# A hybrid decoder step: GpSimd's two-operand work in the recurrence on VectorE

## The chip, the cores and the metric

The kernel runs on one core of one Trainium2 chip. The metric is the device time of one execution in microseconds (us), the median of several runs. The core's engines are TensorE (PE; its weight loads are listed apart as PEld), VectorE (DVE), ScalarE (ACT), GpSimd (POOL) and SyncE (SP), which issues the DMAs. Each engine takes its own instructions in a fixed order and waits on semaphores for the others.

## The reference

One inference step of a one-layer decoder over a prompt of 1024 tokens and 8 sample tokens, width 1024. All weights and activations are float32. Cut to what matters here:

```python
zall = xn @ w_in                      # 45 column blocks of 128
# time-mix branch, 8 heads x 64, a recurrence over the tokens with a 64x64 state S per head
def _wkv_step(S, inp):
    r, w, k, v, aa, bb = inp
    sa = einsum('bhij,bhj->bhi', S, aa)
    S = S * w[:, :, None, :] + sa[..., :, None] * bb[..., None, :] + v[..., :, None] * k[..., None, :]
    y = einsum('bhij,bhj->bhi', S, r)
    return S, y
y_b = gelu(u) * chunk_spatial(layer_norm(gelu(vb)))       # gMLP branch
merged = sigmoid(m_a) * ((y_a * silu(g_a)) @ w_br_a) + sigmoid(m_b) * ((y_b * silu(g_b)) @ w_br_b)
h = h + merged @ w_out
h = h + sigmoid(h @ w_ple_gate + b) * (p @ w_ple)
y = rms_norm(h) * final_g
```

The prompt's state starts at zero. Each sample token has a stored state of its own and makes one step of the recurrence ("decode").

## The kernel before

**Low parts.** Every large product is made of three matmuls. A float32 operand is split into a rounded high part, which ScalarE copies out, and a low part, which is the operand less the high part: a subtraction with two operands in SBUF. `split` (L111 to L114) does both and takes the engine of the subtraction as an argument. `load_w` (L116 to L127) fetches a weight block in pieces of 128x512, splits each and gives the subtraction to GpSimd. The tags `whi` and `wlo` have three buffers each, and so has `wraw`, the piece as it was fetched. A piece of the next weights can therefore be split only when TensorE has used the last of a buffer.

**Stages.** First the norms, the per-layer projection and the v columns (0 to about 100 us). Then the recurrence (about 100 to 830 us): the prompt is cut into 8 units (4 pairs of heads x 2 halves of the tokens), and each unit into 8 chunks of 64 tokens. Last the merge, the output projection, the gate and the final norm (830 us to the end).

**The recurrence.** For unit `un`, `stage_e` makes the factors: decays, normed keys `e_kn`, key products `m1b` (L663 for the r rows, L665 for the keys), `e_bk`, and splits `e_kp` into `e_rkh` and `e_rkl`. `stage_s` solves a triangular system in 31 steps, each a product into `xtmp` (L737) and an addition into `xg` (L739) on VectorE. `stage_c` is the chain from chunk to chunk: TensorE `pt` (L827), ScalarE `e`, TensorE `pt` (L833), ScalarE `vsb`, TensorE `p3b` (L838), VectorE `vsb` (a SCALAR_TENSOR_TENSOR, recorded at the helper's line L791), and again. `stage_t` finishes a unit.

**Fill.** Between the chain's steps TensorE is given other matmuls: 41 blocks of `w_in` (`zblock`, `ga`, `ugb`, `mgate`) and 8 blocks of `w_br_b` (`br_b`), three matmuls for each 128 rows, all at L138. `Stream.pick` loads the weights of the next block while the present one runs. `ugb` multiplies its result into `mx` (L904). `load_ya` and `load_yb` fetch the branches' inputs back and split them (`xlo`). `lora_w` splits a small weight (`llo`), the branch L530 splits `la`. `sample` is the decode: its four state tiles go in two rounds, in each one on GpSimd and one on VectorE (`E_`, L1015 to L1029).

**Order.** The order on each engine is fixed when the program is built, by a planner that gives an engine the ready instruction of the best priority, by reckoned durations. Instructions of `stage_c` and `stage_t` go through `Boost` and come ahead of all others. The rest goes by the order in which it was written (priority 100000 and up), so a low part has no rank of its own. On the chip an engine keeps that order whatever the durations are.

Of the kernel before, what the change touches and what calls it, by code (L numbers as in the profile page):

```python
# [27 lines left out]
CH = 64  # L28
# [26 lines left out]
def body(tc, A):  # L55
# [7 lines left out]
    with ExitStack() as top:  # L63
# [47 lines left out]
        def split(hi, lo, eng, raw=None):  # L111
            raw = f32(lo) if raw is None else raw
            S.copy(hi, raw)  # L113
            eng.tensor_tensor(lo, raw, f32(hi), ALU.subtract)  # L114

        def load_w(src, nk, pool=None):  # L116
            out = []
            for k0 in range(0, nk, 4):
                n = min(4, nk - k0)
                x = k0 if pool else ""  # L120
                hi = (pool or wp).tile([P, 4, P], F32R, tag=f"whi{x}", name="whi")[:, :n]
                lo = (pool or wp).tile([P, 4, P], F32R, tag=f"wlo{x}", name="wlo")[:, :n]
                raw = (pool or wp).tile([P, 4, P], F32, tag="wraw", name="wraw", bufs=WRAW)[:, :n]
                SY.dma_start(raw, src[:, k0:k0 + n, :])
                split(hi, lo, G, raw)
                out += [(hi[:, k], lo[:, k]) for k in range(n)]
            return out  # L127

# [370 lines left out]
        def zblock(b, mk):  # L499
            def gen(w):  # L500
                z = mk()
                G.memset(z[:, 0:1], 0.0)

                def ev(n, ns, ps):
                    S.copy(z[:, 1 + n * W3:1 + (n + 1) * W3], ps)
                yield from mm_block(w, xhi, xlo, ev)

                def mix():
                    G.tensor_copy(zsh[:, b], z[:, TP:TP + NB + 1])
                    if b < 12:  # L510
                        zt.setdefault(b % 4, {})[b // 4] = z
                    mu = col("mu", b)
                    for n in (2, 1, 0):
                        c0 = 1 + n * W3
                        c1 = c0 + W3
                        d = r2.tile([P, W3], F32, tag="zd", name="zd")
                        e1 = min(c1, TP + 1)
                        V.tensor_tensor(d[:, :e1 - c0], z[:, c0 - 1:e1 - 1], z[:, c0:e1], ALU.subtract)
                        if n == 2:
                            V.tensor_tensor(d[:, e1 - c0:], shs[:, b], z[:, TP + 1:], ALU.subtract)  # L520
                        V.scalar_tensor_tensor(z[:, c0:c1], d, mu, z[:, c0:c1], ALU.mult, ALU.add)
                    if b < 12:
                        G.tensor_copy(zsm[:, (1, 0, 2)[b // 4], b % 4], z[:, TP + 1:])
                    else:
                        S.activation(z[0:64, 1:], z[0:64, 1:], AF.Tanh)
                        G.tensor_copy(wdas, z[:, TP + 1:])
                        for q, x, E_ in ((Q[0], lw, V), (Q[1], la, G)):
                            oq = Q[1 - q.start // 64]
                            S.copy(x[q], z[q, 1:])
                            E_.tensor_tensor(x[oq], z[q, 1:], f32(x[q]), ALU.subtract)  # L530
                if b // 4 != 1:
                    return mix
                mix()
            j, x = b % 4, b // 4
            go = {0: lambda: st.r_seen >= 2 * j, 1: lambda: st.k_seen >= 2 * j, 2: lambda: st.c_seen >= 2 * j - 4,
                  3: lambda: True}[x]
            st.add(("z", b), b, gen, ready=go if x != 1 else lambda: st.it >= 2 * j - 3, go=go)
# [38 lines left out]
        def lora_w(j):  # L576
# [4 lines left out]
                    SY.dma_start(raw[Q[h], x], A["wup"][x * 64:x * 64 + 64, js])  # L581
            S.copy(lhi, raw)
            for x in range(2):
                G.tensor_tensor(llo[Q[x], x], raw[Q[x], x], f32(lhi[Q[x], x]), ALU.subtract)

        sgat, zt, ut, fin_s, tl = {}, {}, {}, {}, {}
        ybh, ybl = xhi[:, 0:4], xlo[:, 0:4]
# [2 lines left out]
        def stage_e(un):  # L590
# [54 lines left out]
            V.scalar_tensor_tensor(kp, zr[:, hs], col("r_k", j), kp, ALU.mult, ALU.mult)  # L645
            rkh = re_.tile([P, HT], F32R, tag="e_i", name="e_rkh")
            rkl = re_.tile([P, HT], F32R, tag="e_a", name="e_rkl")
            split(rkh, rkl, G, kp)
            yield YE[2]
            st.until(("z", 8 + j))  # L650
            if un == 0:
# [5 lines left out]
            for b0 in (0, 4):  # L657
# [2 lines left out]
                    yield 1  # L660
                for h in range(2):
                    q = Q[h]
                    G.tensor_tensor(m1[q, cs, h, RC[h]], c64(zr[q, hs])[:, cs], p65[q, cs, 1:], ALU.mult)  # L663
                    for b in range(2):
                        (G, V)[h].tensor_tensor(kord(m1[q, cs, h, AC[h]], b), perm(c64(kn[q])[:, cs], b),  # L665
                                                perm(p65[q, cs, 0:CH], b), ALU.mult)
                if b0:
                    st.r_seen += 1
                ps = aps().rearrange("p (c h x) -> p c h x", h=2, x=CH)
# [222 lines left out]
        def ugb(j, part):  # L892
            def gen(w):
# [3 lines left out]
                def ev(n, ns, ps):  # L897
# [3 lines left out]
                    else:  # L901
                        S.activation(ue, ps, AF.Tanh, scale=0.5)
                        V.scalar_tensor_tensor(ue, ue, 1.0, ps, ALU.add, ALU.mult)
                    G.tensor_tensor(mx[:, ns], mx[:, ns], ue, ALU.mult)  # L904
                yield from mm_block(w, xhi, xlo, ev)
                SY.dma_start(d_yb[j], mx)
            st.add(("u", j, part), (17 if part == 0 else 25) + j, gen)
# [20 lines left out]
        def sample():  # L928
# [83 lines left out]
            yl = sa_(P, 32, tag="s_yl")  # L1012
            for r in range(2):
                it = []
                for x, E_ in enumerate((G, V)):  # L1015
                    isl, s_ = sst[2 * r + x]
                    t_ = re_.tile([P, 8, HD], F32, tag=("e_a", "e_p")[x], name="s_t")
                    sa8 = r2.tile([P, 8], F32, tag="s_sa", name="s_sa")
                    E_.tensor_tensor(t_, s_, bi(lv[:, NKK]), ALU.mult)
                    it.append((E_, isl, s_, t_, sa8))  # L1020
                yield YS[0]
                for E_, isl, s_, t_, sa8 in it:
                    V.tensor_reduce(sa8, t_, AX.X, ALU.add)
                    E_.tensor_tensor(s_, s_, bi(lv[:, WV]), ALU.mult)
                    E_.tensor_tensor(t_, bj(sa8), bi(lv[:, BV]), ALU.mult)
                    E_.tensor_tensor(s_, s_, t_, ALU.add)
                    E_.tensor_tensor(t_, bj(lvv[:, isl]), bi(lv[:, KP]), ALU.mult)
                    E_.tensor_tensor(s_, s_, t_, ALU.add)
                    E_.tensor_tensor(t_, s_, bi(lv[:, RV]), ALU.mult)  # L1029
                yield YS[1]  # L1030
                for E_, isl, s_, t_, sa8 in it:
                    V.tensor_reduce(yl[:, isl], t_, AX.X, ALU.add)
                yield 1
                while r == 0 and st.cdone < 7 * HCH + 3:
                    yield 1
# [36 lines left out]
        def load_ya(n):  # L1072
            ns = slice(n * W3, min((n + 1) * W3, TP))
            st.load = SY.dma_start(f32(yal[:, :3, ns]), d_ya[:3, :, ns].rearrange("k p t -> p k t")).ins
            for k in range(3):
                st.later.append(lambda k=k, ns=ns: split(yah[:, k, ns], yal[:, k, ns], G))

        def load_yb(n):
            V, S, G_ = (Boost(e) for e in (nc.vector, nc.scalar, nc.gpsimd))
            ns = slice(n * W3, (n + 1) * W3)  # L1080
            SY.dma_start(f32(ybl[:, :, ns]), d_yb[:, :, ns].rearrange("k p t -> p k t"))
            for k in range(4):
                S.copy(ybh[:, k, ns], f32(ybl[:, k, ns]))
                (G_ if k == 1 else V).tensor_tensor(ybl[:, k, ns], f32(ybl[:, k, ns]), f32(ybh[:, k, ns]), ALU.subtract)

        def br_b(j):
            def gen(w):
# [11 lines left out]
        fill += [lambda j=j: mgate(37 + j, d_mb[j]) for j in range(KD)]  # L1099
        fill += [lambda j=j: mgate(29 + j, d_ma[j]) for j in range(KD)]  # L1100

        tc.cur_priority = 100000
        boost[0] = 50000
        zblock(12, lambda: re_.tile([P, T + 1], F32, tag="zr", name="wda"))
# [61 lines left out]
            pass  # L1166
        repool.__exit__(None, None, None)
        rw.close()
        use_pmm(4)

        tr2 = top.enter_context(tc.tile_pool(name="tr2", bufs=2))
# [219 lines left out]
```

## Time and profile before

| what | value |
|---|---|
| median of 3 runs | 1077.36 us (1076.85 to 1077.84) |
| the profiled execution | 1079.88 us, of which the profiled span is 1078.0 us |
| TensorE busy | 1016.7 us (94%) |
| VectorE busy | 655.1 us (61%) |
| GpSimd busy | 471.6 us (44%) |
| ScalarE busy | 449.3 us (42%) |
| granted TensorE clock, mean | 0.978 of full |

A busy figure sums the instructions' own durations; an instruction that is held by something inside it counts as busy. Idle time of an engine is put down to what released the instruction behind it. A group of instructions is written as line, engine, operation, output<-inputs, shapes, count, then busy time and mean duration, then the idle time before them.

### The profile page before, as it was taken

Reading aid. Unit: us, or ns where it says so; the run is one execution under the profiler, and the core shown is the slowest. Engines: PE = TensorE matmul, PEld = TensorE weight load, DVE = VectorE, ACT = ScalarE, POOL = GpSimd, SP = SyncE. Lnnn points to the kernel's source line nnn. Section 1 sums busy time; section 2 is a strip of 40 time slices with the busy share of each in tenths; the row PEclk is TensorE's granted clock in tenths of the full one; section 3 lists DMA queues with packets and bytes.
Section 4 is the critical chain, followed back from the end, with each engine's and each line's share of the span. In section 5 each row is a group of like instructions: output and inputs, shape, how many; then the busy total and the mean of one; then the engine's idle time right before and its main releaser. Section 6 shows DMA issues by size and latency. Waiting matters only on the chain. (4 is left out here: it accounts for less than half of the span.)

```text
span 1078.0 us, 17989 instructions
## 1 busy us (share of the span) xinstructions
PE 1016.7 (94%) x6590; PEld 978.4 (91%) x6590; DVE 655.1 (61%) x1487; ACT 449.3 (42%) x1087; POOL 471.6 (44%) x484
## 2 busy tenths in 40 slices
PE   8889999899798999989998999999899999999996
PEld 8768898899798899989998999989799999999995
DVE  6898565847648768577476583563876551114544
ACT  4531334245364453555444545434532232225431
POOL 2462665444364343343414333334943674453213
PEclk9999999999899999999998999999899999999997
DMA  9811412152224231132232332422765763224204
GB/s 277 243 51 48 145 40 58 40 131 83 79 78 151 79 86 61 47 103 56 79 110 49 105 101 70 134 86 41 266 206 179 240 231 118 79 83 133 80 1 157
DMA packets 95224, 118.72 MB, mean 110 GB/s; under 512 B 40672, under 2 KB 61024, under 8 KB 95136
## 3 DMA queue, kind: packets, MB, share of 16 engines
q1 hardware_dynamic: 95136, 117.57, 35.5%
q8 instruction: 52, 0.85, 0.3%
q14 instruction: 36, 0.29, 0.1%
HBM read 84.75 MB, written 32.25 MB: 109 GB/s over the span
## 5 line engine op out<-in xcount | busy, mean ns | idle before, releaser
L138 PE MATMUL mm<-xhi,wlo 128*128 128x344 f32 x1176 | 388.2, 330 | 8.0 <-POOL wlo L114 6.2
L138 PE MATMUL mm<-xlo,whi 128*128 128x344 f32 x1176 | 389.3, 331 | 0.9 <-DVE xlo L791 0.8
L138 PE MATMUL mm<-xhi,whi 128*128 128x344 f32 x1176 | 388.7, 331 | 0.4 <-DVE mb L1092 0.3
L114 POOL TENSOR_TENSOR wlo<-wraw,whi 128x512 fp32r<-128x512 f32 x130 | 171.2, 1319 | 217.6 <-ACT whi L113 215.6
L138 PEld LDWEIGHTS mm<-xhi,wlo 128*128 128x128 f32 x1176 | 225.1, 191 | 10.5 <-POOL wlo L114 7.3
L138 PEld LDWEIGHTS mm<-xlo,whi 128*128 128x128 f32 x1176 | 224.9, 191 | 3.0 <-DVE xlo L791 1.7
L138 PEld LDWEIGHTS mm<-xhi,whi 128*128 128x128 f32 x1176 | 224.9, 191 | 2.6 <-DVE mb L1092 0.6
L113 ACT CAST whi<-wraw 128x512 fp32r<-128x512 f32 x130 | 80.2, 619 | 61.8 <-PE mm L138 44.4
L737 DVE TENSOR_TENSOR xtmp<-nb,xg 128x48 f32<-128x48 f32 (+23 forms) x248 | 70.6, 285 | 20.4 <-DMA nb<-d_n 13.6
L739 DVE TENSOR_TENSOR xg<-xg,xtmp 128x48 f32<-128x48 f32 (+23 forms) x248 | 78.0, 315 | 7.6 <-DVE xtmp L737 0.2
L791 ACT ACTIVATE sp<-vsb,pc 64x64 f32<-64x64 f32 x128 | 44.2, 345 | 69.6 <-DVE vsb L791 67.7
L791 DVE SCALAR_TENSOR_TENSOR vsb<-p3b,pc,sp 64x64 f32<-64x64 f32 x112 | 31.6, 282 | 57.5 <-PE p3b L838 55.3
L827 PEld LDWEIGHTS pt<-vsb,m1b 128*128 128x128 f32 x256 | 37.9, 194 | 28.0 <-DVE vsb L791 27.5
L138 PE MATMUL mm<-hlo,whi 128*128 128x388 f32 (+1 forms) x192 | 62.0, 323 | 0.0
L138 PE MATMUL mm<-hhi,whi 128*128 128x388 f32 (+1 forms) x192 | 61.7, 321 | 0.0
L138 PE MATMUL mm<-hhi,wlo 128*128 128x388 f32 (+1 forms) x192 | 61.7, 321 | 0.0
L138 PE MATMUL mm<-mgl,whi 128*128 128x344 f32 x192 | 61.4, 320 | 0.2 <-POOL mgl L1188 0.2
L827 PE MATMUL pt<-vsb,m1b 128*128 128x64 f32 x256 | 40.4, 275 | 22.4 <-DVE vsb L791 22.4
L138 PE MATMUL mm<-mgh,whi 128*128 128x344 f32 x192 | 61.3, 319 | 0.0
L138 PE MATMUL mm<-mgh,wlo 128*128 128x344 f32 x192 | 61.3, 319 | 0.0
L1202 DVE SCALAR_TENSOR_TENSOR h<-mm,xres 128x344 f32<-128x344 f32 x24 | 12.4, 517 | 75.0 <-PE mm L138 72.6
L791 ACT COPY vsb<-pt 64x64 f32<-64x64 f32 x128 | 26.5, 207 | 43.7 <-PE pt L833 41.7
(297 smaller groups left out, 1881.5 us busy)
## 6 DMA issues: line engine op xcount, KB each, us to landing
wraw<-w_in SPq DMA_DIRECT2D x82, 256.0 KB, 2.8
d_ple<-st_ple SPq DMA_DIRECT2D x8, 516.0 KB, 3.4
d_yb<-mx SPq DMA_DIRECT2D x8, 516.0 KB, 2.8
d_mb<-st_m SPq DMA_DIRECT2D x8, 516.0 KB, 3.4
d_ma<-st_m SPq DMA_DIRECT2D x8, 516.0 KB, 4.1
mb<-d_mb SPq DMA_DIRECT2D x8, 516.0 KB, 4.3
d_tb<-mb SPq DMA_DIRECT2D x8, 516.0 KB, 4.9
ma<-d_ma SPq DMA_DIRECT2D x8, 516.0 KB, 5.3
```

The lines of the kernel that those rows point to most:

```text
L113: S.copy(hi, raw)
L114: eng.tensor_tensor(lo, raw, f32(hi), ALU.subtract)
L138: PE.matmul(ps, l, r, start=(k == 0 and i == 0), stop=(k == nk - 1 and i == 2))
L737: V.tensor_tensor(tv, row.unsqueeze(2).broadcast_to([P, 2, na, w]), xg[:, :, :na, s:s + 1].broadcast_to([P, 2, na, w]), ALU.mult)
L739: V.tensor_tensor(xg[:, :, :na, s + 1:], xg[:, :, :na, s + 1:], tv, ALU.add)
L791: r = f(*a, **k)
L827: PE.matmul(pt[:, 0, h], m1[:, c, h], vs[:, c, h], start=True, stop=True)
L1202: V.scalar_tensor_tensor(h[:, j, ns], ps, 0.25, xr[:, ns], ALU.mult, ALU.add)
```

## The change

All low parts, branch products, key products and the decode's second state that GpSimd made between the start of the recurrence and its end are given to VectorE. `load_w` takes its engine from a list that is set to VectorE ahead of the recurrence and back to GpSimd behind it, so the weight blocks of the last stage stay as they were. What stays on GpSimd in the recurrence: the powers (`rpow`, L101), the scaling of `e_s` (L605), memsets, and copies.

```diff
+        sub = [G]
...
-                split(hi, lo, G, raw)
+                split(hi, lo, sub[0], raw)
...
-                        for q, x, E_ in ((Q[0], lw, V), (Q[1], la, G)):
+                        for q, x in ((Q[0], lw), (Q[1], la)):
...
-                            E_.tensor_tensor(x[oq], z[q, 1:], f32(x[q]), ALU.subtract)
+                            V.tensor_tensor(x[oq], z[q, 1:], f32(x[q]), ALU.subtract)
...
-                G.tensor_tensor(llo[Q[x], x], raw[Q[x], x], f32(lhi[Q[x], x]), ALU.subtract)
+                V.tensor_tensor(llo[Q[x], x], raw[Q[x], x], f32(lhi[Q[x], x]), ALU.subtract)
...
-            split(rkh, rkl, G, kp)
+            split(rkh, rkl, V, kp)
...
-                    G.tensor_tensor(m1[q, cs, h, RC[h]], c64(zr[q, hs])[:, cs], p65[q, cs, 1:], ALU.mult)
+                    V.tensor_tensor(m1[q, cs, h, RC[h]], c64(zr[q, hs])[:, cs], p65[q, cs, 1:], ALU.mult)
                     for b in range(2):
-                        (G, V)[h].tensor_tensor(kord(m1[q, cs, h, AC[h]], b), perm(c64(kn[q])[:, cs], b),
-                                                perm(p65[q, cs, 0:CH], b), ALU.mult)
+                        V.tensor_tensor(kord(m1[q, cs, h, AC[h]], b), perm(c64(kn[q])[:, cs], b),
+                                        perm(p65[q, cs, 0:CH], b), ALU.mult)
...
-                    G.tensor_tensor(mx[:, ns], mx[:, ns], ue, ALU.mult)
+                    V.tensor_tensor(mx[:, ns], mx[:, ns], ue, ALU.mult)
...
-                for x, E_ in enumerate((G, V)):
+                for x in range(2):
...
-                    E_.tensor_tensor(t_, s_, bi(lv[:, NKK]), ALU.mult)
+                    V.tensor_tensor(t_, s_, bi(lv[:, NKK]), ALU.mult)
...
-                st.later.append(lambda k=k, ns=ns: split(yah[:, k, ns], yal[:, k, ns], G))
+                st.later.append(lambda k=k, ns=ns: split(yah[:, k, ns], yal[:, k, ns], V))
...
-                (G_ if k == 1 else V).tensor_tensor(ybl[:, k, ns], f32(ybl[:, k, ns]), f32(ybh[:, k, ns]), ALU.subtract)
+                V.tensor_tensor(ybl[:, k, ns], f32(ybl[:, k, ns]), f32(ybh[:, k, ns]), ALU.subtract)
...
+        sub[0] = V
         tc.cur_priority = 100000
         boost[0] = 50000
...
         rw.close()
+        sub[0] = G
         use_pmm(4)
```

## Rows read from the trace of the kernel before

**Rows 1.** Busy by stretch: PE, PEld, DVE, ACT, POOL, granted clock, DMA.

```profile
100.00:215.00 115.00, 106.14 (x696) 101.58 (x695) 75.66 (x152) 42.06 (x91) 60.47 (x77) 0.99 0.25 77
215.00:745.00 530.00, 505.66 (x3467) 491.35 (x3467) 337.56 (x893) 256.99 (x699) 209.29 (x231) 0.98 0.31 88
745.00:830.00 85.00, 76.72 (x477) 72.97 (x476) 63.90 (x107) 33.93 (x93) 49.17 (x36) 0.96 0.57 189
...
880.00:1078.00 198.00, 187.73 (x1197) 186.72 (x1195) 64.89 (x113) 62.78 (x119) 75.42 (x69) 0.97 0.30 101
```

**Rows 2.** Waits of TensorE over the span: us in total, times, longest us.

```profile
PE pt L827 <- DVE vsb L791: 22.4, 19, 5.5
PE mm L138 <- POOL wlo L114: 6.2, 4, 2.4
...
PE aa L671 <- DVE e_bk L641: 3.7, 1, 3.7
...
PE mm L138 <- POOL zr L502: 1.8, 1, 1.8
```

**Rows 3.** Timeline of TensorE, its longest wait: start, us, what, idle before.

```profile
283.50 0.90 PE L827 MATMUL pt<-vsb,m1b 128*128 128x64 f32 x3 [5.51 <-DVE vsb L791]
```

**Rows 4.** Timeline of VectorE in the 11.5 us ahead of that wait's end.

```profile
273.51 2.17 DVE L739 TENSOR_TENSOR xg<-xg,xtmp 128x48 f32<-128x48 f32 x1
275.61 1.77 DVE L641 SCALAR_TENSOR_TENSOR e_bk<-e_a,e_i 128x512 f32<-128x512 f32 x1
...
278.86 1.41 DVE L665 TENSOR_TENSOR m1b<-e_kn,e_p 64x128 f32<-64x128 f32 x1
280.30 1.16 DVE L737 TENSOR_TENSOR xtmp<-nb,xg 128x48 f32<-128x48 f32 x1
281.50 0.83 DVE L739 TENSOR_TENSOR xg<-xg,xtmp 128x48 f32<-128x48 f32 x1
...
283.17 0.59 DVE L791 SCALAR_TENSOR_TENSOR vsb<-p3b,pc,sp 64x64 f32<-64x64 f32 x2
```

**Rows 5.** Timeline of GpSimd in the same stretch.

```profile
271.60 1.44 POOL L663 TENSOR_TENSOR m1b<-zr,e_p 64x256 f32<-64x256 f32 x2 [2.20 <-DVE xg L739]
273.11 1.58 POOL L665 TENSOR_TENSOR m1b<-e_kn,e_p 64x128 f32<-64x128 f32 x2
...
275.54 1.28 POOL L114 TENSOR_TENSOR wlo<-wraw,whi 128x512 fp32r<-128x512 f32 x1
...
281.36 0.90 POOL L904 TENSOR_TENSOR mx<-mx,ue 128x344 f32<-128x344 f32 x1
```

**Rows 6.** TensorE by stretch, behind and ahead of that wait: busy (matmuls), clock, DMA.

```profile
283.50:289.50 6.00, 6.00 (x23) 0.50 0.61 191
269.50:275.50 6.00, 6.00 (x44) 1.00 0.00 0
```

**Rows 7.** Groups of GpSimd by shape, 100 to 815 us.

```profile
L114 POOL TENSOR_TENSOR wlo<-wraw,whi 128x512 fp32r<-128x512 f32 x87 | 115.1, 1326 | 152.4 <-ACT whi L113 150.8 <-PE mm L138 0.9
...
L101 POOL TENSOR_TENSOR s_pool<-s_pool,mhalf 128x16 f32<-128x16 f32 x2 | 5.9, 2952 | 11.7 <-DVE s_pool L925 11.7
```

**Rows 8.** Groups of the page, the two operations of the triangular solve.

```profile
L737 DVE TENSOR_TENSOR xtmp<-nb,xg 128x48 f32<-128x48 f32 (+23 forms) x248 | 70.6, 285 | 20.4 <-DMA nb<-d_n 13.6
L739 DVE TENSOR_TENSOR xg<-xg,xtmp 128x48 f32<-128x48 f32 (+23 forms) x248 | 78.0, 315 | 7.6 <-DVE xtmp L737 0.2
```

**Rows 9.** Single lines of VectorE: duration ns min/median/max, starts, forms.

```profile
L739 DVE TENSOR_TENSOR xg<-xg,xtmp x248: 166/224/2174, 190.3 to 725.9; 128x48 f32<-128x48 f32 x12, 128x54 f32<-128x54 f32 x8, 128x84 f32<-128x84 f32 x8, 128x56 f32<-128x56 f32 x8
...
L665 DVE TENSOR_TENSOR m1b<-e_kn,e_p x32: 384/788/1976, 150.6 to 670.8; 64x128 f32<-64x128 f32 x32
...
L641 DVE SCALAR_TENSOR_TENSOR e_bk<-e_a,e_i x8: 682/1116/1774, 151.4 to 644.3; 128x512 f32<-128x512 f32 x8
...
L700 DVE TENSOR_TENSOR w3b<-aa,mka x32: 405/417/419, 165.5 to 683.2; 64x256 f32<-64x256 f32 x32
...
L518 DVE TENSOR_TENSOR zd<-zr x12: 498/508/1412, 143.3 to 573.8; 128x344 f32<-128x344 f32 x8, 128x336 f32<-128x336 f32 x4
```

More of the change, by code (lines that the diff above doesn't have):

```diff
@@ L1018, in sample @@
                     sa8 = r2.tile([P, 8], F32, tag="s_sa", name="s_sa")
-                    E_.tensor_tensor(t_, s_, bi(lv[:, NKK]), ALU.mult)
-                    it.append((E_, isl, s_, t_, sa8))
+                    V.tensor_tensor(t_, s_, bi(lv[:, NKK]), ALU.mult)
+                    it.append((isl, s_, t_, sa8))
                 yield YS[0]
-                for E_, isl, s_, t_, sa8 in it:
+                for isl, s_, t_, sa8 in it:
                     V.tensor_reduce(sa8, t_, AX.X, ALU.add)
[L1024 to L1029, printed above, removed]
+                    V.tensor_tensor(s_, s_, bi(lv[:, WV]), ALU.mult)
+                    V.tensor_tensor(t_, bj(sa8), bi(lv[:, BV]), ALU.mult)
+                    V.tensor_tensor(s_, s_, t_, ALU.add)
+                    V.tensor_tensor(t_, bj(lvv[:, isl]), bi(lv[:, KP]), ALU.mult)
+                    V.tensor_tensor(s_, s_, t_, ALU.add)
+                    V.tensor_tensor(t_, s_, bi(lv[:, RV]), ALU.mult)
                 yield YS[1]
-                for E_, isl, s_, t_, sa8 in it:
+                for isl, s_, t_, sa8 in it:
                     V.tensor_reduce(yl[:, isl], t_, AX.X, ALU.add)
@@ L1075, in load_ya @@
             for k in range(3):
-                st.later.append(lambda k=k, ns=ns: split(yah[:, k, ns], yal[:, k, ns], G))
+                st.later.append(lambda k=k, ns=ns: split(yah[:, k, ns], yal[:, k, ns], V))
         def load_yb(n):
-            V, S, G_ = (Boost(e) for e in (nc.vector, nc.scalar, nc.gpsimd))
+            V, S = (Boost(e) for e in (nc.vector, nc.scalar))
             ns = slice(n * W3, (n + 1) * W3)
```

## The prediction, made before the changed kernel was run

> **What bounds the kernel now.** I read the busy times by stretch first. TensorE is busy for 505.66 of 530 us in the heart of the recurrence, 76.72 of 85 in its last unit and 187.73 of 198 in the last stage [rows 1]. VectorE stands at 64% of the recurrence (337.56 of 530) and GpSimd at 39%, so neither is the bound by its mean. The change can act only through what TensorE loses between 100 and 830 us: its waits, and the low clock that follows long waits.
>
> The waits come second. 22.4 us in 19 waits go to the chain's VectorE step `vsb`, 6.2 us to low parts of weights from GpSimd, 3.7 us to `e_bk`, 1.8 us to a memset on GpSimd [rows 2]. The granted clock is the second loss: 0.99 of 115 us, 0.98 of 530 and 0.96 of 85 [rows 1] make 1.2 + 10.6 + 3.4 = 15 us. Behind the longest wait the clock reads 0.50 (1.2 GHz), and TensorE makes 23 matmuls in 6 us where it had made 44 at the full 2.4 GHz [rows 6].
>
> Third, the timeline ahead of that longest wait. TensorE stood from 277.99 to 283.50 [rows 3], for a `vsb` that started on VectorE at 283.17 [rows 4]. The timeline shows no idle time of VectorE before it, but its instructions were swollen: an addition of 48 elements took 2.17 us, and the same line takes 0.22 us at the median; `e_bk` took 1.77 against a shortest of 0.68, a key product 1.41 against 0.38, two more of the solve 1.16 and 0.83 [rows 4, 9]. In each of these GpSimd was at a two-operand instruction of its own [rows 5]; one `mx` and two splits like those shown are left out there. The excess of these five is 1.95 + 1.09 + 1.03 + 0.94 + 0.61 = 5.6 us. So VectorE and GpSimd hold one another when both read two operands from SBUF, and the planner's order, in which `vsb` stands behind four steps of the solve that rank below it, fits durations that didn't come about.
>
> **What the change takes away.** The same excess over the whole recurrence: the solve's 496 instructions are busy for 70.6 + 78.0 = 148.6 us [rows 8]; at the median of 0.224 they would take 111 [rows 9], so 38 us are holding. Of the 32 key products on VectorE half take 0.79 or more against 0.38, at least 6 us more; of the eight `e_bk` half take 1.12 or more against 0.68, at least 2 us [rows 9]. That makes 46 us. My estimate for all two-operand lines of VectorE, mean less shortest form by form in the same way, is about 90 us. What stays on GpSimd reads little (powers of 8 or 16 elements, copies), so I take nearly all of it as gone.
>
> **What it adds.** By uncontended VectorE durations [rows 9]: 0.69 us for 128x512 (the shortest `e_bk`, rounded up), 0.51 for 128x344, 0.42 for 64x256, 0.38 for a key product. There are 87 low parts of weights [rows 7] and 3 more before 100 us, 8 `rkl`, and 14 instructions of the decode: 112 x 0.69 = 77 us. 24 `mx` and 12 `xlo`: 36 x 0.51 = 18. 32 r products x 0.42 = 13, 32 key products x 0.38 = 12. `la` and eight `llo`, not seen at this price: about 4, between 3 and 6. Together 125 us, where GpSimd spent 115.1 us on the 87 alone [rows 7]. VectorE's busy time should so rise by 125 - 90 = 35 us, or by up to 79 if only the 46 shown come off.
>
> **Part a, the chain's waits.** In the longest, 5.6 us of excess go. What GpSimd did in that stretch [rows 5] comes to VectorE: two r products, two key products, three splits (two of weights, one `rkl`) and two `mx`, 0.84 + 0.77 + 2.07 + 1.02 = 4.7 us. If all of it stands ahead of `vsb`, the wait shrinks by 0.9 of 5.5; if none, it is gone. Splits and `mx` rank below `vsb` and are not wanted soon, so the planner can put them behind; the products' results are wanted soon. Carried over to all 22.4 us the gain lies between 16% and 100%, 3.7 to 22.4. I take **-10**, short of the middle (13), because the other 18 waits last 0.94 us in the mean ((22.4 - 5.5) / 18) [rows 2] and need not have this cause.
>
> **Part b, waits for GpSimd itself.** 6.2 + 1.8 us [rows 2]. A split costs 0.69 in place of 1.33 [rows 7, 9], which alone gives 4 x 0.64 = 2.5 us. Two powers of the decode hold GpSimd for 5.9 us [rows 7], and splits queue behind them; on VectorE they don't. Bounds -2.5 and -8; I take **-5**. **Part c**, `e_bk`: 0.4 (median less shortest) to 3.7; **-1**.
>
> **Part d, the clock.** 15 us are at stake, and they follow long waits. Bounds 0 and -15; with the few longest waits cut I take **-5**.
>
> **Part e, new waits.** A split waits for ScalarE's `whi`, which waits for TensorE to leave a buffer; on GpSimd such waiting came to 150.8 us ahead of the 87 splits and cost nothing [rows 7]. On VectorE the chain's `vsb`, the solve and the key products queue behind it, and TensorE's `pt` waits for `vsb`. Lower bound 0: the waiting falls where VectorE would have been idle. Upper bound: it hurts in the 64% in which VectorE has work, 96 us, of which as much reaches TensorE as of the 90 us of holding now (22.4 of 90, a quarter): 24 us. The decode's second state adds 14 x 0.69 = 9.7 us to the last unit, where VectorE is busy for 63.9 of 85 us [rows 1]; that fits, and is cut from nothing. I take **+8**, a third of the bound: TensorE's progress sets both the waits for `whi` and those of the chain, so an order that holds for one mostly holds for the other. The DMAs are all on SP's queue and move past no other; `wraw` is freed sooner by the shorter split, if VectorE comes to it in time. Work before 57 us and behind 830 us is the same.
>
> **The sum.** -10 - 5 - 1 - 5 + 8 = -13. Against the profiled execution's 1079.9 this is 1067; that execution lay 2.5 us above the median of the runs, so against the median of 1077.4 I say **1064**. The ends of the parts: -3.7 - 2.5 - 0.4 - 0 + 24 = +17, and -22.4 - 8 - 3.7 - 15 + 0 = -49.
>
> **Rivals.** *Break-even.* In the loaded stretch 4.7 us come for the 5.6 that go. If the low ends of a to d hold (-6.6) and the new waits are as I took them (+8), the time is 1079, within a few us of now. For it: the ledger of the one stretch. Against: the added work can be ranked behind the chain, the holding could not.
>
> *VectorE held at the front of its queue (slower).* One mechanism: a split stands on VectorE waiting for `whi`, with `vsb` behind it. Price 24 us from above, less 6.6 from the low ends: +17, **1094**, and somewhere from 1083 up if half as much reaches TensorE. It decides from the point at which the new waits exceed the 21 us of parts a to d. For it: 150.8 us of waiting move onto the chain's engine, which is full in the stretches that matter. Against: VectorE has 36% idle time to wait in. The Trainium skill ("Perfetto Trace Analysis", Optimizing Scalar/DVE Operations) speaks on this side: where VectorE is saturated, giving work to ScalarE or even GpSimd may pay, and it adds that the two share a read port, so that it may not. By its first half this rival comes true, by the second the forecast; the swollen rows agree with the second.
>
> *Everything gives way.* The long waits were all holding, and the clock stays up: -49 with a few us of new waits, about 1035. Against: 16.9 of the chain's 22.4 us lie in waits of 0.94 us in the mean, about one uncontended instruction of VectorE.
>
> *The change doesn't do what it says*: what is left on GpSimd still holds VectorE. Then the 46 to 90 us stay and 125 come on top; this ends with the slower rival and is counted there.
>
> **Chances.** Forecast (1050 to 1074) 0.46, break-even (1072 to 1081) 0.22, slower 0.27, everything 0.05. About 0.2%, 2.2 us, is what a measurement of this kernel can tell from no change, so faster means below 1075.2 and slower above 1079.5. Of break-even 0.09 lies below, 0.11 within, 0.02 above. Faster 0.46 + 0.05 + 0.09 = 0.60, same 0.11, slower 0.29. The range 1046 to 1092 leaves out the greater part of the last rival (0.04), the upper part of the slower one (0.10) and little else. The likeliest case's own range is 1050 to 1074.
>
> **What will show it.** In the profile of the changed kernel the median and mean of the solve's lines should agree near 0.22 us, `e_bk` should take 0.68, and a split 0.69. VectorE should be busy for 655 + 35 = 690 us (734 if little holding goes), GpSimd for at least 115 less. The waits for `vsb` should fall from 22.4 to about 12, none over 3 us; those for GpSimd's splits should be gone in the recurrence, and waits for VectorE's splits stand at under 8. I am wrong if `vsb` comes late behind splits that stand idle for `whi`, or if TensorE waits for VectorE's `wlo` as long as it had waited for GpSimd's and the chain together.

## The result and the profile after

The changed kernel takes **1035.8 us** (1035.14 to 1037.66), against 1077.1 us for the kernel before on the same chip: a ratio of 0.9621, with a 95% interval of 0.9604 to 0.9637. The profiled span falls from 1078.0 to 1034.1 us, by 43.9. The direction was forecast; the size was not. The forecast was 1064, and the time lies 10 us below the stated range. It lies where the rival "everything gives way" had put it.

Engines of the changed kernel over the span: busy us, share, instructions.

```profile
PE 1000.4 (97%) x6590; PEld 967.8 (94%) x6590; DVE 667.3 (65%) x1708; ACT 450.7 (44%) x1087; POOL 231.5 (22%) x263
```

The 43.9 us have two parts. TensorE's idle time, span less busy time, falls from 61.3 (1078.0 - 1016.7) to 33.7 (1034.1 - 1000.4), by 27.6. Its busy time for the same 6590 matmuls falls by 16.3, from 1016.7 to 1000.4. Most of that is the clock: its mean rises from 0.978 to 0.990, which is worth some 12 us (an estimate, 1016.7 x (1 - 0.978 / 0.990)). What the other 4 us are is not shown.

The third figure is the one to stop at. VectorE received some 125 us of work and is busy for only 12 us more, 667.3 for 655.1. Part of that is only the way busy time counts: the records of neighbouring instructions overlap by about 0.1 us, and an overlap counts once. Summed instruction by instruction, VectorE's durations rise by 30.7 us, from 699.3 to 730.0, and the work that came makes 125.4 of them. So about 95 us of what the profile of the kernel before had called busy was holding (125.4 - 30.7).

The changed kernel by stretch, in the columns of [rows 1]. The first three stretches are those of before; the last one ends with the span.

```profile
100.00:215.00 115.00, 109.83 (x738) 106.36 (x737) 83.41 (x208) 46.33 (x100) 21.87 (x35) 1.00 0.26 78
215.00:745.00 530.00, 521.73 (x3625) 509.54 (x3623) 371.54 (x1086) 275.80 (x748) 54.97 (x80) 0.99 0.35 103
745.00:830.00 85.00, 81.94 (x519) 80.52 (x518) 58.20 (x116) 25.67 (x62) 35.16 (x31) 0.98 0.63 213
...
880.00:1034.00 154.00, 143.66 (x924) 143.09 (x922) 57.51 (x99) 51.48 (x98) 51.92 (x47) 0.97 0.28 93
```

Against [rows 1], TensorE makes 3625 matmuls in the middle stretch where it made 3467. GpSimd's busy time there falls from 209.29 to 54.97, and VectorE's rises by only 34 (337.56 to 371.54), although the stretch holds more work than before. The first matmul of the output projection comes at 834.5 instead of 877.4, so the gain is made before the last stage. Some 4 us of it are made before the recurrence: the last matmul of the v columns ends at 90.2 us instead of 94.4. About 2 of these go with a stretch of low clock at 10 to 14 us, which e3 and e8 have too and the changed kernel has not; nothing that the change moves runs so early. TensorE's waits for VectorE's `acc` in the first stage, 5.3 us before and 3.6 now, are 5.0 or more in every kernel that leaves the first three splits, from 57 us on, with GpSimd (e3 and e7).

Waits of TensorE in the changed kernel: total us, times, longest us. They answer to [rows 2].

```profile
PE mm L140 <- DVE wlo L114: 4.7, 3, 1.9
PE pst L263 <- DVE acc L260: 3.6, 3, 1.5
PE pt L829 <- DVE vsb L793: 3.5, 8, 0.9
PE fst L1252 <- ACT gq L1233: 2.1, 2, 1.5
PE pt L835 <- ACT e L793: 1.9, 5, 0.6
PE aa L1062 <- DVE s_ys L927: 1.7, 1, 1.7
PE aa L695 <- DVE zv L690: 1.6, 1, 1.6
```

The chain's waits for `vsb` are 3.5 us in 8 where they were 22.4 in 19, and the longest is 0.9 instead of 5.5. The waits for GpSimd's splits (6.2), for `zr` (1.8) and for `e_bk` (3.7) are gone. The one new wait that counts is 4.7 us for splits that are now VectorE's.

Groups of the changed kernel: instructions, then busy us and mean ns, then the idle time ahead of them. They answer to [rows 7, 8]; the line numbers are two higher.

```profile
L114 DVE TENSOR_TENSOR wlo<-wraw,whi 128x512 fp32r<-128x512 f32 x90 | 61.7, 689 | 27.4 <-ACT whi L113 23.2
L739 DVE TENSOR_TENSOR xtmp<-nb,xg 128x48 f32<-128x48 f32 (+23 forms) x248 | 54.5, 220 | 13.6 <-DMA nb<-d_n 7.5
L741 DVE TENSOR_TENSOR xg<-xg,xtmp 128x48 f32<-128x48 f32 (+23 forms) x248 | 54.6, 220 | 6.2
```

Single lines of VectorE, in the columns of [rows 9].

```profile
L741 DVE TENSOR_TENSOR xg<-xg,xtmp x248: 168/219/419, 181.5 to 685.7; 128x48 f32<-128x48 f32 x12, 128x54 f32<-128x54 f32 x8, 128x84 f32<-128x84 f32 x8, 128x56 f32<-128x56 f32 x8
L643 DVE SCALAR_TENSOR_TENSOR e_bk<-e_a,e_i x8: 683/689/695, 143.9 to 607.8; 128x512 f32<-128x512 f32 x8
L667 DVE TENSOR_TENSOR m1b<-e_kn,e_p x64: 355/394/454, 143.6 to 635.0; 64x128 f32<-64x128 f32 x64
```

This is the mark of the mechanism. The solve's addition had 224 ns at the median but 315 in the mean, and 2174 at the longest [rows 8, 9]; now mean and median agree at 0.22 us, and the longest is 419. `e_bk` runs from 683 to 695 ns where it ran from 682 to 1774. A 128x512 subtraction takes 0.689 us on VectorE; on GpSimd it took 1.326 [rows 7].

GpSimd's side of it, from the kernel before: duration in ns (min/median/max) of its splits of weights.

```profile
L114 POOL TENSOR_TENSOR wlo<-wraw,whi x130: 1255/1289/1721, 57.3 to 1035.6; 128x512 fp32r<-128x512 f32 x130
```

These 130 hardly swell. The prediction says that the two engines hold one another; by these records the holding fell almost wholly on VectorE.

The stretch that stalled before, on the changed kernel's VectorE: start, us, what. It goes from the same `e_bk` as in [rows 4] to the chain's next `vsb`.

```profile
262.20 0.20 DVE L741 TENSOR_TENSOR xg<-xg,xtmp 128x48 f32<-128x48 f32 x1
262.32 0.69 DVE L643 SCALAR_TENSOR_TENSOR e_bk<-e_a,e_i 128x512 f32<-128x512 f32 x1
...
263.42 0.52 DVE L906 TENSOR_TENSOR mx<-mx,ue 128x344 f32<-128x344 f32 x1
...
264.51 0.69 DVE L114 TENSOR_TENSOR wlo<-wraw,whi 128x512 fp32r<-128x512 f32 x1
265.11 0.21 DVE L739 TENSOR_TENSOR xtmp<-nb,xg 128x56 f32<-128x56 f32 x1
265.24 0.41 DVE L665 TENSOR_TENSOR m1b<-zr,e_p 64x256 f32<-64x256 f32 x1
265.57 0.68 DVE L114 TENSOR_TENSOR e_rkl<-e_kp,e_rkh 128x512 fp32r<-128x512 f32 x1
266.20 0.60 DVE L793 SCALAR_TENSOR_TENSOR vsb<-p3b,pc,sp 64x64 f32<-64x64 f32 x2
...
267.23 0.20 DVE L741 TENSOR_TENSOR xg<-xg,xtmp 128x56 f32<-128x56 f32 x1
```

Before, `vsb` started 7.6 us behind the start of `e_bk` (283.17 - 275.61). Now it is 3.9 us (266.20 - 262.32), 3.7 less, with four instructions of GpSimd's old work in between. TensorE comes for this `vsb` at 267.95, 1.15 us after it is done (266.20 + 0.60), and without a gap: here the chain waits for TensorE. The swelling of the four instructions that [rows 4] shows in that stretch, `e_bk` among them, comes to as much (1.09 + 1.03 + 0.94 + 0.61 = 3.7). But the planner's order has changed too: of the eight instructions of the solve that stood between `e_bk` and `vsb`, seven now stand behind `vsb`, and so do two key products, which makes room for most of the added work. Whether the gain is the order's or the holding's is one thing the experiments had to tell.

### The profile page after: what moved, and what is told of

Read it like the earlier page. It is cut to its first block, busy times and chain, and to the rows that moved or that the text cites. A ratio compares the mean times of both kernels' runs of the same rounds, so it can differ in the third digit from the quotient of the medians.

```text
span 1034.1 us, 17902 instructions
## 1 busy us (share of the span) xinstructions
PE 1000.4 (97%) x6590; PEld 967.8 (94%) x6590; DVE 667.3 (65%) x1708; ACT 450.7 (44%) x1087; POOL 231.5 (22%) x263
## 4 chain that ended last, share of the span: by engine, by line
PE 82%; DVE 9%; ACT 4%; DMA 2%; issue 2%; POOL 1%; SPq 0%; POOLq 0%; DVEq 0%; ACTq 0%
PE mm L140 65%; PE psv L291 3%; PE pt L829 2%; PE p3b L840 2%; PE aa L695 2%; PE pt L835 1%; DVE xtmp L739 1%; DVE xg L741 1%; PE aa L766 1%; DVE yc L793 1%; PE aa L774 1%; DMA nb<-d_n 1%; ACT yc L793 1%; DVE xr L275 1%; DVE acc L260 1%
## 5 line engine op out<-in xcount | busy, mean ns | idle before, releaser
L114 POOL TENSOR_TENSOR wlo<-wraw,whi 128x512 fp32r<-128x512 f32 x40 | 53.5, 1338 | 124.7 <-ACT whi L113 124.4
L114 DVE TENSOR_TENSOR wlo<-wraw,whi 128x512 fp32r<-128x512 f32 x90 | 61.7, 689 | 27.4 <-ACT whi L113 23.2
L793 ACT ACTIVATE sp<-vsb,pc 64x64 f32<-64x64 f32 x128 | 44.2, 345 | 46.9 <-DVE vsb L793 44.9
L739 DVE TENSOR_TENSOR xtmp<-nb,xg 128x48 f32<-128x48 f32 (+23 forms) x248 | 54.5, 220 | 13.6 <-DMA nb<-d_n 7.5
L140 PE MATMUL mm<-mgh,whi 128*128 128x344 f32 x192 | 61.3, 319 | 0.0
L140 PE MATMUL mm<-mgh,wlo 128*128 128x344 f32 x192 | 61.3, 319 | 0.0
L140 PE MATMUL mm<-mgl,whi 128*128 128x344 f32 x192 | 61.3, 319 | 0.0
L741 DVE TENSOR_TENSOR xg<-xg,xtmp 128x48 f32<-128x48 f32 (+23 forms) x248 | 54.6, 220 | 6.2
```

The source lines that it names most:

```text
L140: PE.matmul(ps, l, r, start=(k == 0 and i == 0), stop=(k == nk - 1 and i == 2))
L739: V.tensor_tensor(tv, row.unsqueeze(2).broadcast_to([P, 2, na, w]), xg[:, :, :na, s:s + 1].broadcast_to([P, 2, na, w]), ALU.mult)
L741: V.tensor_tensor(xg[:, :, :na, s + 1:], xg[:, :, :na, s + 1:], tv, ALU.add)
L793: r = f(*a, **k)
```

## The experiments

**The theory**: GpSimd's reads of two operands hold VectorE's, and the held time reaches TensorE. **The rivals**: the gain comes from the splits being shorter on VectorE (0.69 for 1.33 us), so that TensorE gets its weights sooner; or it comes from the new order. Ratios are to the kernel before on the same chip, with a 95% interval. "Solve" is the mean ns of its product and of its addition.

| kernel | ratio | span, us | VectorE busy, us | GpSimd busy, us | solve, ns |
|---|---|---|---|---|---|
| before | 1 | 1078.0 | 655.1 | 471.6 | 285 / 315 |
| changed | 0.9621 [0.9604, 0.9637] | 1034.1 | 667.3 | 231.5 | 220 / 220 |
| e1, changed, GpSimd repeats the splits | 0.998 [0.9959, 1.0002] | 1075.5 | 721.4 | 399.6 | 263 / 269 |
| e2, changed, GpSimd only writes | 0.9617 [0.9587, 0.9646] | 1036.5 | 666.4 | 380.8 | 219 / 219 |
| e3, before, GpSimd writes and doesn't read | 0.9743 [0.9709, 0.9777] | 1050.4 | 606.6 | 462.8 | 248 / 245 |
| e4, before, only the splits of weights moved | 0.9689 [0.9654, 0.9724] | 1046.7 | 662.7 | 358.6 | 244 / 246 |
| e5, e2 with reads for the fills | 0.9837 [0.9803, 0.9872] | 1059.6 | 705.4 | 400.8 | 254 / 253 |
| e6, e5's work on VectorE | 0.9722 [0.9685, 0.9759] | 1046.8 | 728.7 | 238.6 | 219 / 217 |
| e7, all moved but the splits of weights | 0.968 [0.9641, 0.9719] | 1042.7 | 664.1 | 353.1 | 278 / 249 |
| e8, changed, early stage too | 0.9586 [0.955, 0.9622] | 1033.8 | 666.8 | 209.0 | |
| e9, changed, again | 0.9615 [0.9587, 0.9644] | 1033.3 | 666.1 | 231.7 | |
| e10, e8 again | 0.9591 [0.9561, 0.9622] | 1035.4 | 668.7 | 208.6 | |
| e11, e5 with half the reads | 0.9653 [0.9625, 0.968] | 1038.2 | 684.7 | 337.5 | 231 / 238 |

**e1: the reads put back on GpSimd, unused.** In the changed kernel GpSimd makes each subtraction of a weight block once more, in two halves, into a tile that nobody reads.

```diff
+                    for i in (0, 2):
+                        G.tensor_tensor(dum[0], raw[:, i:i + 2], f32(hi[:, i:i + 2]), ALU.subtract)
```

> The changed kernel, but GpSimd makes each of the 90 weight subtractions of the recurrence once more, in two halves, into a tile that nobody reads. The order of TensorE's and VectorE's instructions is that of the changed kernel but for 5 and 6 lines. Nothing waits for GpSimd's copy except the buffer that it reads. Theory 'holding' (VectorE and GpSimd stop one another when each reads two operands from SBUF): the solve's instructions go from a mean of 220 ns to 260 or more, waits for vsb come back, 1050 to 1062 us. Rival 'latency' (what cost time was GpSimd's slow delivery, and splits queued behind its other work): 1034 to 1039 us, since nothing needs GpSimd's result. Rival 'order' (the planner's new order made the gain): 1034 to 1039 us, since the order stays.

The whole gain is gone: 1077.7 us, beyond the range that holding was given. But the run has a fault of its own, which TensorE's waits in it show.

```profile
PE mm L143 <- ACT whi L113: 10.0, 1, 10.0
PE mm L143 <- DVE wlo L114: 9.0, 4, 3.6
PE pt L832 <- DVE vsb L796: 8.0, 12, 2.4
```

The wait of 10.0 us for ScalarE's `whi` ends at 121 us and exists in no other kernel here. GpSimd's repeat reads `wraw`, and so keeps that buffer from the next fetch. This run therefore mixes holding with later loads, and the next two kernels avoid that.

**e2 and e5: the same GpSimd time with and without reads.** Both copy one element of `whi` behind each split, which ties them to the same moment. Then e2 fills a tile with zeros four times, and e5 multiplies a constant tile by itself twice. The fetched piece is not kept. The copy keeps `whi` until GpSimd comes to it, but alike in both: ScalarE waits 8.7 us in all for that in e2 and 9.5 in e5.

```diff
+                    G.tensor_copy(dum[0][:, 0, :1], f32(hi)[:, 0, :1])
+                    for _ in range(4):                                # e2
+                        G.memset(dum[0], 0.0)
+                    for _ in range(2):                                # e5, in its place
+                        G.tensor_tensor(dum[0], mka, mka, ALU.mult)
```

> As e1, but in place of the repeated subtraction GpSimd copies one element and then fills the same unread tile four times with zeros, about 1.2 us for each weight piece, so GpSimd is as long busy but reads nothing. Holding: 1034 to 1040 us, the solve's mean stays at 220 ns. If any work on GpSimd disturbs VectorE, or what delays is the power and the scaling queued behind it: 1045 us or more, like e1.

> As e2, but in place of the four fills GpSimd multiplies a constant table by itself twice, 128x256 each, for each weight piece: about 1.35 us that read two operands from SBUF and hold no buffer that others need (in e1 the repeated subtraction held the fetched piece, and TensorE lost 10.0 us in one wait for that at about 113 us). TensorE's order is that of e2 in every line, VectorE's but for 2. Holding: what e1 lost beyond that one wait and its low clock, so 1052 to 1065 us, with the solve's mean near 260 ns. Latency or order: 1038 to 1042 us, as e2.

GpSimd is busy for 380.8 and 400.8 us, nearly alike, and the order on TensorE is the same in both. Yet e2 runs like the changed kernel and e5 takes 23.1 us of span more. One stretch of the solve on VectorE shows why, first in e2 (GpSimd's line, then VectorE's) and then in e5.

```profile
204.45 1.42 POOL L131 MEMSET dum<- 128x256 f32 x4
...
204.62 0.22 DVE L743 TENSOR_TENSOR xtmp<-nb,xg 128x60 f32<-128x60 f32 x1
204.88 0.22 DVE L745 TENSOR_TENSOR xg<-xg,xtmp 128x60 f32<-128x60 f32 x1
205.13 0.22 DVE L743 TENSOR_TENSOR xtmp<-nb,xg 128x54 f32<-128x54 f32 x1
```

```profile
212.93 1.31 POOL L131 TENSOR_TENSOR dum<-mka 128x256 f32<-128x256 f32 x2
...
213.05 0.57 DVE L743 TENSOR_TENSOR xtmp<-nb,xg 128x60 f32<-128x60 f32 x1
213.66 0.66 DVE L745 TENSOR_TENSOR xg<-xg,xtmp 128x60 f32<-128x60 f32 x1
214.35 0.22 DVE L743 TENSOR_TENSOR xtmp<-nb,xg 128x54 f32<-128x54 f32 x1
```

Beside four fills the two instructions of the same step take 0.22 us each. Beside two multiplications they take 0.57 and 0.66, and the next one, which starts 0.11 us after GpSimd is done (212.93 + 1.31), takes 0.22 again: VectorE is let go only when each multiplication ends. The Trainium skill ("SBUF — State Buffer", Who interferes with whom) says this: an instruction of VectorE with two inputs from SBUF contends with one of GpSimd that reads SBUF, but not with one that only writes it, and the loser blocks fully. These rows agree on both halves. So neither the order nor GpSimd's being busy makes the difference; its reads do. The price: e5's VectorE is busy for 39.0 us more, and TensorE ends 23.1 us later, 0.59 us for one of holding.

How it reaches TensorE is less simple than the theory has it. TensorE's longest sum of waits and those for the chain, in e2, then in e5:

```profile
PE mm L144 <- DVE wlo L114: 3.7, 3, 2.1
...
PE pt L833 <- DVE vsb L797: 3.4, 7, 1.1
```

```profile
PE mm L144 <- DVE wlo L114: 7.6, 4, 3.4
PE pt L833 <- DVE vsb L797: 5.5, 10, 1.6
```

Of the 23.1 us, 9.5 are busy time (1000.9 to 1010.4; the mean clock is 0.984 for 0.990), and 13.6 are idle. Of the idle time the chain's `vsb` has only 2.1 and the splits have 3.9; the rest lies in single waits of other kinds.

**e3: the reads taken away in the old order.** In the kernel before, GpSimd writes zeros where it had subtracted, for the weights of the recurrence.

```diff
-                split(hi, lo, G, raw)
+                if rec[0]:                      # in the recurrence
+                    S.copy(hi, raw)
+                    G.tensor_copy(lo[:, 0, :1], f32(hi)[:, 0, :1])
+                    for _ in range(2):
+                        G.memset(f32(lo), 0.0)
+                else:
+                    split(hi, lo, G, raw)
```

> The kernel before, but in the recurrence GpSimd fills the 90 low parts of weights with zeros (one element copied from the high part, two fills of 128x512, together about 1.2 us against 1.33) in place of the subtraction: the weights' low parts are left out of the products. Everything stays on the engine it was on, and the order on TensorE and VectorE is that of the kernel before but for 10 and 12 lines. Holding: the part of the excess that came from the weights goes, about half, so 1050 to 1063 us. Latency: 1073 to 1078 us, as GpSimd delivers as late as before. Order: 1077 us.

Engines of e3, and TensorE's two longest sums of waits.

```profile
PE 1005.2 (96%) x6590; PEld 971.2 (92%) x6590; DVE 606.6 (58%) x1487; ACT 449.4 (43%) x1087; POOL 462.8 (44%) x664
...
PE pt L835 <- DVE vsb L799: 12.2, 15, 3.3
PE mm L146 <- POOL wlo L131: 6.5, 4, 2.4
```

VectorE does exactly the work of before, in an order that differs in a dozen places, and is busy for 48.5 us less (655.1 to 606.6). GpSimd is nearly as busy as it was (462.8 for 471.6). The chain's waits fall from 22.4 to 12.2, and the span by 27.6: 0.57 us for one of holding, close to e5's 0.59 from the other direction. The waits for GpSimd's low parts are as they were, 6.5 us for 6.2. For two thirds of the gain (2.57 of 3.79%) both rivals fall: the weights came no sooner, and the order was the old one. For the last third no run tells the holding that e3 leaves from the new order. e3 also makes TensorE multiply by zeros, which no run sets apart in its busy time (1005.2 for 1016.7 us); e2 against e5 is free of that.

**e6: the price of work itself.** What e5 gave to GpSimd, VectorE does.

```diff
-                        G.tensor_tensor(dum[0], mka, mka, ALU.mult)
+                        V.tensor_tensor(dum[0], mka, mka, ALU.mult)
```

> As e5, but VectorE does the copy and the two multiplications of the constant table, about 0.9 us for each of 90 weight pieces, some 80 us more of busy time on the engine of the chain, and nobody reads the result. My part e said that work which queues on VectorE reaches TensorE at a quarter: plus 20 us on 1036, so 1056. If the planner ranks such work behind the chain and it fills idle time: 1036 to 1044 us. Compared with e5 it says whether a microsecond of VectorE's own work or one of holding costs more.

The added group in e6 (the copy moved with it), one of the solve, and the chain's waits.

```profile
L131 DVE TENSOR_TENSOR dum<-mka 128x256 f32<-128x256 f32 x180 | 76.6, 426 | 2.2
L745 DVE TENSOR_TENSOR xg<-xg,xtmp 128x48 f32<-128x48 f32 (+23 forms) x248 | 53.8, 217 | 4.8
...
PE pt L833 <- DVE vsb L797: 2.9, 7, 0.5
```

VectorE is busier than in any other kernel here, 728.7 us, yet e6 is 12.8 us of span faster than e5, where VectorE stands at 705.4. Some 90 us of instructions (76.6 and 13.2 for the copies) cost 10.3 us over e2, 0.11 us each. At 1049.7 us it lies below the 1056 of the quarter and above the range for work that only fills idle time. The waits for `vsb` stay at 2.9. My reading is that the planner reckons with work that is VectorE's own and sets it behind the chain; it can't reckon with holding.

**e4 and e7: either half alone.** e4 is the kernel before with only the weights' splits moved; e7 is the changed kernel with only these left on GpSimd.

```diff
+        sub[0] = V        # e4: all that is changed of the kernel before
...
-        sub[0] = V        # e7: against the changed kernel
+        sub[0] = G
```

> The kernel before with the one edit that the 90 weight subtractions of the recurrence are VectorE's; products, mx, decode and the rest stay on GpSimd. Holding: about half of the 41 us, 1052 to 1062 us, with the solve's mean near 250 ns. Latency: nearly all of the gain, under 1045 us, since the splits are what TensorE waits for. My own sum (part a by the ledger of one stretch) would put it at 1068.

> The changed kernel with the one part undone: the 90 weight subtractions of the recurrence stay on GpSimd, products, mx, decode and the rest are VectorE's. With weights alone moved (e4) 29 of the 41 us came. If the parts add up, the rest is worth 12 us: 1064 to 1068 us. If a microsecond of holding costs the more the more there is of it, the two parts alone make less than the whole: 1066 to 1074. If either part alone breaks the long waits: 1050 to 1058.

The chain's waits and the solve's addition in e4, then in e7.

```profile
L741 DVE TENSOR_TENSOR xg<-xg,xtmp 128x48 f32<-128x48 f32 (+23 forms) x248 | 61.0, 246 | 6.8
...
PE pt L829 <- DVE vsb L793: 11.8, 13, 3.6
```

```profile
L741 DVE TENSOR_TENSOR xg<-xg,xtmp 128x48 f32<-128x48 f32 (+23 forms) x248 | 61.8, 249 | 6.8
...
PE pt L829 <- DVE vsb L793: 5.8, 11, 0.9
```

Each half alone takes off a part of the swelling (0.246 and 0.249 us in the mean, against 0.315 and 0.220), and each brings over four fifths of the gain: 3.11 and 3.20% of 3.79. They don't add. e4's 1048.2 us lie between its two ranges and e7's 1044.8 below all of its three. What holding is left when either half is gone costs little, and the first half taken away, whichever it is, brings the most.

The chain's waits don't go by the amount of holding alone. Summed by instruction, e3, e4, e7 and e1 show 46, 48, 52 and 54 us more of it than the changed kernel. The waits for `vsb` are 12.2 and 11.8 us in e3 and e4, where products, `mx` and decode are GpSimd's, and 5.8 and 8.0 in e7 and e1, where they are VectorE's. Whether that is the order, or that the products on GpSimd fall at worse moments for the chain, no run tells.

**e11: half of e5's reads.** One multiplication in place of two.

```diff
-                    for _ in range(2):
+                    for _ in range(1):
                         G.tensor_tensor(dum[0], mka, mka, ALU.mult)
```

> As e5 with one multiplication of the constant table for each weight piece in place of two, so half the two-operand reading on GpSimd (90 instructions in place of 180). e5 put 39 us on VectorE's busy time over e2 and 23 us on the span, 0.59 us for each us held. If that price holds at any dose: 18 to 22 us on VectorE, 10 to 14 us on the time, a ratio of 0.971 to 0.976. If little holding is absorbed and only much of it hurts: under 5 us, 0.967 or less.

Against e2, VectorE is busy for 18.3 us more and the span is 1.7 us longer. By the ratios it is 0.36%, 4 us, with intervals that overlap, so this first half can't be told from no cost. The second half of the reads brings 20.7 us more of holding (684.7 to 705.4) and 21.4 us of span, 1.84% by the ratios, with intervals far apart. So one us of holding has no fixed price: the first 18 us cost at most little, 0.1 each by the spans and 0.2 by the ratios, the next 21 about 1 each. Nor does the price simply rise with the amount: e7, with 52 us more of holding than the changed kernel, is 8.6 us slower than it (with 62 us less work of its own on VectorE), and e5, with 39, is 25.5 us slower. My explanation is that the order has slack in front of each wait, which small delays use up, and that long waits bring the low clock with them (its mean is 0.990 in e2, 0.989 in e11 and 0.984 in e5). The clocks are shown. The slack is argued: no run measured it.

**e8 to e10: is there more of the same?** In the stage ahead of the recurrence GpSimd still takes half the splits of the v weights and the norm's low parts. e8 and e10 give these to VectorE too; e9 is the changed kernel beside e10.

```diff
-                    split(h, l, (G, V)[kk], raw)
+                    split(h, l, V, raw)
...
-                G.tensor_tensor(xlo[:, :, ts_], xr, f32(xhi[:, :, ts_]), ALU.subtract)
+                V.tensor_tensor(xlo[:, :, ts_], xr, f32(xhi[:, :, ts_]), ALU.subtract)
```

> The changed kernel, and in the first stage as well GpSimd's low parts (nine of 128x1024 and four of 128x512) are VectorE's. There VectorE is busy for 87 of 100 us and TensorE waits for it 3.6 us (acc) and 0.8 us for GpSimd. Holding: the swollen steps of the first stage shrink by as much as comes, or more, 1031 to 1036 us. If VectorE is full there: 1037 to 1045 us.

> The changed kernel once more, beside e10 and e11 on one chip: a ratio of 0.960 to 0.964 to the kernel before.

> The kernel of e8 once more, beside the changed kernel. In e8 TensorE reached the output projection at 832.3 us of the span against 834.5 in the changed kernel, but a low clock of 19.9 us at the very end took that back. If the two us are real and the end varies by itself: a ratio 0.001 to 0.003 below e9's. If not: the same as e9.

The splits of the v weights on VectorE: the changed kernel (e9), where GpSimd makes four others, then e10.

```profile
L114 DVE TENSOR_TENSOR wlo_v<-wrawv,whi_v 128x512 fp32r<-128x512 f32 x4 | 6.6, 1661 | 2.6 <-ACT whi_v L113 2.6
```

```profile
L114 DVE TENSOR_TENSOR wlo_v<-wrawv,whi_v 128x512 fp32r<-128x512 f32 x8 | 5.4, 690 | 1.7 <-ACT whi_v L113 1.7
```

The small case shows the holding again: four splits beside GpSimd's four cost VectorE 6.6 us, and all eight alone cost it 5.4. In time it is not settled. Both pairs put the variant ahead, by 0.35% (e8 against the first run of the changed kernel) and 0.24% (e10 against e9), but the intervals overlap each time, and e10's profiled span is 2.1 us longer than e9's.

## Why the prediction was right in kind and wrong in size

**What held.** The mechanism, read from one stretch of two timelines [rows 3 to 5], is the one that e2, e3 and e5 show, on VectorE's side; GpSimd's own splits hardly swelled. The marks that were named ahead came too. The solve stands at 0.22 us, `e_bk` and a split at 0.689, GpSimd is busy for 240 us less (at least 115 had been said), and waits for VectorE's splits come to 4.7 us (under 8). The amount also held: 90 us of holding were estimated from the shortest durations form by form, and 95 went. VectorE's busy time is 667 where 690 was said, because the sum left out the overlap of neighbouring records (699.3 - 655.1 = 44.2 us before, 730.0 - 667.3 = 62.7 after).

**The failed steps are the sizes of the parts**, of d and a above all. Part d came out 11.3 us beyond what was taken and part a 8.9, then e 5.0, b 3.0 and c 2.7: together the 30.9 us between -13 and -43.9. In a to d a value near the middle or the cautious end was taken, and each came out near its far bound or, by TensorE's busy time, beyond it:

| part | bounds | taken | measured |
|---|---|---|---|
| a, waits for `vsb` | -3.7 to -22.4 | -10 | -18.9 (22.4 to 3.5) |
| b, waits for GpSimd | -2.5 to -8 | -5 | -8.0 (both gone) |
| c, `e_bk` | -0.4 to -3.7 | -1 | -3.7 (gone) |
| d, clock | 0 to -15 | -5 | -16.3 (TensorE's busy time; -10.2 of it is low clock in the recurrence) |
| e, new waits | 0 to +24 | +8 | +4.7 for splits; all the rest that changed, -1.7 |

The measured column sums to -43.9, since the first three and e make the 27.6 us of idle time. The rest in e is what 27.6 leaves (18.9 + 8.0 + 3.7 - 4.7 = 25.9).

**Part d, where -5 had no working.** Summed over stretches of 2 us, the low clock cost 15.3 us between 100 and 830 us before and costs 5.1 between 100 and 787 now: 10.2 less, inside the bounds and twice what was taken. In the kernel before each of the six stretches of low clock in the recurrence stands at a wait of 1.5 to 5.5 us, four of them for `vsb`, one for `e_bk` and one for a split. No wait for `vsb` or `e_bk` of that length is left, and three such stretches are. The other 6 us of busy time are not the recurrence's low clock: 1.7 are the stretch at 10 to 14 us, and the rest is open.

**Part a, the argument behind -10.** The prediction reckoned that the 18 shorter waits, 0.94 us in the mean, need not come from holding. They went all the same: 8 are left, of 0.4 us in the mean. That holding alone had made them is not shown, since 39 us of it put back into the new order (e5) bring the waits to 5.5 us and not to 22.4. It reckoned also with the added 4.7 us of work ahead of the same `vsb`. In the changed kernel four such instructions stand there (0.52 + 0.69 + 0.41 + 0.68 = 2.3 us), seven of the solve and two key products have gone behind, and TensorE doesn't wait.

**One ratio for two things.** Part e took it that a quarter of holding reaches TensorE (22.4 of 90), and carried VectorE's own waiting over at the same rate. Measured, holding costs 0.57 to 0.59 (e3, e5) and own work 0.11 (e6). The ratio of a quarter counted only the waits named `vsb` and left out the low clock behind them and the waits for `e_bk`. With the measured prices the sum would have been 95 x 0.57 less 125 x 0.11, 54 - 14 = 40 us of gain, against 43.9. That this comes so near is in part luck, since the price of holding went from 0.1 to 1 (e11).

**The chances.** Parts a to d were treated as if each could fall short by itself. Parts a, c and d hang together: the clock falls at the waits, and most of these were for `vsb` and `e_bk`. So "everything gives way" was more likely than four separate chances, and 0.05 was low. That its 1035 was met within 1 us is in part luck, as some 4 us were gained ahead of the recurrence, which no part had in it. Part b has a cause of its own: in e3 the waits for GpSimd's splits stayed at 6.5 us with the holding cut by half.

**The rival that would have made it slower**, VectorE held at the front of its queue, had its point of decision in the waiting for `whi`. VectorE's two longest sums of waits in the changed kernel, 100 to 785 us:

```profile
DVE vsb L793 <- PE p3b L840: 32.4, 26, 4.1
DVE wlo L114 <- ACT whi L113: 23.2, 26, 3.1
```

On GpSimd 150.8 us of waiting stood ahead of the splits [rows 7]; on VectorE it is 23.2, in 26 waits, and TensorE lost 4.7. My reading is that VectorE has other instructions ahead of a split and so mostly comes to it when `whi` is there. Its longest sum of waits is for TensorE's `p3b`, as it was before (55.3 us): the chain waits for TensorE. *Break-even* fell with part a's argument. *The change doesn't do what it says* fell with the solve's 0.22 us.

## What to carry to other kernels

Compare mean, median and shortest duration of each form of an engine's instructions before its busy share is believed: held time counts as busy, and VectorE's 655 us here had some 95 us of holding in them that no share showed. Two-operand work in SBUF on GpSimd is not free for being off the critical path; where the chain runs through VectorE it may be cheaper on VectorE itself, since a planner can rank work but not holding, and where work has to stay on GpSimd the kind that only writes did no harm here (e2). A price per microsecond of holding does not carry over: it went from 0.1 to 1 within one pair of experiments. When several terms of a sum have one cause, let them succeed or fail together, and give that case its own chance.

## What the runs showed of the hardware that was not expected

Taking over a line's work from another engine can lower the time that the line costs: eight splits of the v weights on VectorE alone take 5.4 us, four shared with GpSimd 6.6 (e10, e9). Busy time is no order of merit: the kernel before had VectorE at 655.1 us and took 1078.0, e6 had it at 728.7 and took 1046.8.

One instruction of VectorE can be held through several of GpSimd. The addition that took 2.17 us in [rows 4] ran from 273.51 to 275.68, through two key products of GpSimd [rows 5] and this one, which ended at 275.58:

```profile
274.66 0.92 POOL L904 TENSOR_TENSOR mx<-mx,ue 128x344 f32<-128x344 f32 x1
```

The price of holding is strongly uneven: 18.3 us of it cost 1.7 us of span (4 by the ratios), and 20.7 more cost 21.4 (e11, e5). And 16.3 of the 43.9 us came back not as waits but as TensorE's busy time, some 12 of them by its clock, whose mean rose from 0.978 to 0.990 when the chain's waits, at most 5.5 us before, had shrunk to 0.9.
